# One row's load of a row-wise logsumexp dealt unevenly to the DMA engines, 10, 9, 7 and 6 partitions

## The chip, the cores and the metric

The kernel runs on one core of a Trainium2 chip. The metric is the device time of one execution in microseconds (us). The kernel before takes 162.84 us, the median of three runs (162.67 to 163.0); with the profiled run, 162.7, the result below counts four, and the median is 162.77. A run with the profiler gives a page and a trace; the span there, 161.3 us, goes from the first instruction to the last and is somewhat shorter than the device time.

## The reference

```python
def setup_inputs():
    batch, seq, dim = 32, 512, 1024
    return {"x": np.random.randn(batch, seq, dim).astype(np.float32), "axis": -1}

def reference(x, axis):
    x_max = np.max(x, axis=axis, keepdims=True)
    return (x_max.squeeze(axis) + np.log(np.sum(np.exp(x - x_max), axis=axis))).astype(np.float32)
```

64 MB come in, 64 KB go out. Each of the 128 partitions of the on-chip memory takes 128 rows of 1024 numbers. "A row" below means one such row in every partition: 128 pieces of 4 KB.

## The kernel before

The rows come in chunks, 17 loads in all, into a ring of 51 rows. The last four chunks are single rows.

```python
CHUNKS = [
    (4, 4, 1, False), (15, 15, 1, False), (16, 16, 2, False), (16, 16, 2, False),
    (16, 15, 2, False), (14, 14, 2, False), (13, 12, 2, False), (9, 8, 1, False),
    (7, 7, 1, True), (5, 5, 1, True), (4, 4, 1, True), (3, 3, 1, False), (2, 2, 1, True),
    (1, 0, 1, False), (1, 0, 1, False), (1, 0, 1, False), (1, 0, 1, False),
]
# ... cut ...
    def load(i):
        (s, row), r = place[i], CHUNKS[i][0]
        act_wait = max(a for a, _ in busy[s : s + r])
        dve_wait = max(d for _, d in busy[s : s + r])
        if dve_wait:
            nc.sync.wait_ge(dve_done, dve_wait)
        if act_wait:
            nc.sync.wait_ge(act_done, act_wait)
        nc.sync.dma_start(out=ring[:, s : s + r], in_=x_v[:, row : row + r]).then_inc(
            landed[i], 16
        )
# ... cut: ScalarE takes exp of a chunk, VectorE sums it; of the last four rows ScalarE does both ...
        nc.scalar.wait_ge(landed[i], 16)
        for j in range(n_dve, r):
            nc.scalar.activation(
                out=ring[:, s + j], in_=ring[:, s + j], func=Exp, accum_out=total(row + j),
            ).then_inc(act_done, 1)
```

No maximum is subtracted. At the end the kernel counts the sums that lie in a safe range, and only if one does not, a branch runs a second pass. That part is the same in both kernels.

## Time and profile before

| what | value | where it is from |
|---|---|---|
| span | 161.3 us | head of the page |
| share of the DMA queue, sixteen engines | 97.2% | the page's queue table |
| last increment of the loads of chunks 13, 14, 15, 16 | 154.56, 155.85, 157.13, 158.35 us | semaphore increments in the trace |
| start of the exponential on those rows | 155.28, 156.28, 157.28, 158.37 us | the timeline |

A load of 128 partitions leaves sixteen increments of its semaphore in the trace. Linked end to start, the packets of the last four rows form sixteen chains, one for each of the page's sixteen DMA engines, with eight packets and one increment for each row. So a load leaves sixteen time stamps, and ScalarE, which waits for all of them, starts on the last row 0.02 us after its last one (158.37 against 158.35 us). The lines of the page, the chain, the timeline and the tail of the DMA rate are shown in the prediction below.

### The profile page before, as it was taken

The numbers are of one execution on the slowest core, as the hardware profiler recorded it, in microseconds if no ns is written. First come the engines' busy times: TensorE is split into PE (matmuls) and PEld (weight loads), VectorE is DVE, ScalarE is ACT, GpSimd is POOL, SyncE is SP. The second block draws the span as 40 slices with busy tenths as digits, with TensorE's granted clock in tenths as the row PEclk, the third lists the DMA queues.
The fourth block names the chain that finished last, engine by engine and source line by source line (L and its number), as shares of the span: only waits on it lengthen the run. The fifth ranks groups of instructions, "written<-read, shape, count | busy, mean of one in ns | idle before, by whom it ended". The sixth has DMA issues, their size and how long they took to land.

```text
span 161.3 us, 147 instructions
## 1 busy us (share of the span) xinstructions
PE 0.2 (0%) x1; PEld 0.1 (0%) x1; DVE 123.0 (76%) x57; ACT 114.8 (71%) x36; POOL 0.3 (0%) x5
## 2 busy tenths in 40 slices
PE   0000000000000000000000000000000000000000
PEld 0000000000000000000000000000000000000000
DVE  0019000003999999999999699999999999999994
ACT  3080005996079960999419993999199999999996
POOL 0000000000000000000000000000000000000000
DMA  7998899799899899899899999999999999999990
GB/s 266 500 488 381 381 457 520 341 439 520 358 423 520 358 423 520 374 406 520 358 390 455 455 455 439 423 423 423 403 430 439 423 427 420 422 427 421 404 401 34
DMA packets 2593, 67.18 MB, mean 417 GB/s; under 512 B 288, under 2 KB 416, under 8 KB 928
## 3 DMA queue, kind: packets, MB, share of 16 engines
q1 hardware_dynamic: 2592, 67.18, 97.2%
q14 instruction: 1, 0.01, 0.0%
HBM read 67.11 MB, written 0.07 MB: 416 GB/s over the span
## 4 chain that ended last, share of the span: by engine, by line
DMA 51%; DVE 30%; ACT 17%; issue 1%; SPq 0%; PE 0%
DMA ring<-in_x_dram 51%; DVE sums L182 29%; ACT ring L162 15%; ACT ring L189 2%; SPq L122 0%; DVE counts L222 0%; ACT res L131 0%; PE good L227 0%; DVE n_good L232 0%
## 5 line engine op out<-in xcount | busy, mean ns | idle before, releaser
L182 DVE TENSOR_REDUCE sums<-ring 128x8 f32<-128x8192 f32 (+5 forms) x14 | 111.2, 7995 | 36.3 <-ACT ring L162 36.1
L162 ACT ACTIVATE ring<-ring 128x8192 f32<-128x8192 f32 (+7 forms) x18 | 106.1, 5932 | 43.9 <-DMA ring<-in_x_dram 43.9
L169 DVE CUSTOM_DVE_ANT_0 ring<-ring 128x512 f32<-128x512 f32 x18 | 11.2, 688 | 0.0
L189 ACT ACTIVATE ring<-ring 128x1024 f32<-128x1024 f32 x7 | 7.2, 1045 | 0.0
L149 ACT ACT_TABLE_LOAD x1 | 1.3, 1283 | 1.0 <-PEq L312 1.0
L169 DVE DVE_READ_ACCUMULATOR2_ANT sums<- 128x1 f32 x18 | 1.5, 84 | 0.0
L189 ACT ACTIVATION_READ_ACCUMULATOR ring<-ring 128x1 f32 x7 | 1.2, 170 | 0.0
L222 DVE TENSOR_SCALAR counts<-late 128x4 bf16<-128x4 f32 x2 | 0.2, 156 | 0.8 <-ACT res L131 0.8
L206 DVE TENSOR_SCALAR_CACHE_REDUCE marks<-sums 128x124 bf16<-128x124 f32 x2 | 0.5, 280 | 0.0
L131 ACT ACTIVATE res<-sums 128x81 f32<-128x81 f32 (+1 forms) x2 | 0.5, 242 | 0.0
L232 DVE TENSOR_REDUCE n_good<-good 1x1 int32<-1x10 f32 x1 | 0.2, 155 | 0.3 <-PE good L227 0.3
L227 PE MATMUL good<-counts,ones 128*1 128x10 bf16 x1 | 0.2, 168 | 160.0 <-DVE counts L222 160.0
L131 ACT ACTIVATE res<-late 128x4 f32<-128x4 f32 x1 | 0.2, 173 | 0.0
L206 DVE DVE_READ_ACCUMULATOR marks<-sums 128x1 bf16 x2 | 0.2, 86 | 0.0
L227 PEld LDWEIGHTS good<-counts,ones 128*1 128x1 bf16 x1 | 0.1, 79 | 160.0 <-DVE counts L222 160.0
L148 POOL MEMSET ones<- 128x1 bf16 x1 | 0.1, 101 | 0.5 <-POOLq L312 0.5
L312 POOL MEMSET const-bfloat16-1.0<- 128x1 bf16 x1 | 0.1, 101 | 0.0
L312 POOL MEMSET const-uint8-127<- 128x1 uint8 x1 | 0.1, 101 | 0.0
L312 POOL MEMSET const-float32-0.0<- 128x1 f32 x1 | 0.1, 98 | 0.2 <-issue 0.2
L312 POOL MEMSET const-float32-1.0<- 128x1 f32 x1 | 0.1, 98 | 0.0
## 6 DMA issues: line engine op xcount, KB each, us to landing
ring<-in_x_dram SPq DMA_DIRECT2D x1, 7680.0 KB, 25.0
ring<-in_x_dram SPq DMA_DIRECT2D x1, 7168.0 KB, 28.6
ring<-in_x_dram SPq DMA_DIRECT2D x1, 6656.0 KB, 35.7
ring<-in_x_dram SPq DMA_DIRECT2D x1, 4608.0 KB, 20.3
ring<-in_x_dram SPq DMA_DIRECT2D x2, 2048.0 KB, 16.3
ring<-in_x_dram SPq DMA_DIRECT2D x1, 3584.0 KB, 28.3
ring<-in_x_dram SPq DMA_DIRECT2D x1, 2560.0 KB, 27.4
ring<-in_x_dram SPq DMA_DIRECT2D x4, 512.0 KB, 27.0
```

What stands on the lines that cost most here:

```text
L131: nc.scalar.activation(out=res[:, lo:hi], in_=src, func=Ln).then_inc(act_done, 1)
L148: nc.gpsimd.memset(ones, 1.0).then_inc(early, 1)
L149: nc.scalar.preload_act_table_set("natural_log_exp_and_others")
L162: nc.scalar.activation(out=ring[:, s + lo : s + hi], in_=ring[:, s + lo : s + hi], func=Exp).then_inc(act_done, 1)
L169: nc.vector.tensor_tensor_reduce(out=ring[:, s + j, : D // 2], in0=ring[:, s + j, : D // 2], in1=ring[:, s + j, D // 2 :], scale=1.0, scal ...
L182: nc.vector.reduce_sum(out=sums[:, row + lo : row + hi], in_=ring[:, s + lo : s + hi], axis=AX).then_inc(dve_done, 1)
L189: nc.scalar.activation(out=ring[:, s + j], in_=ring[:, s + j], func=Exp, accum_out=total(row + j),).then_inc(act_done, 1)
L206: nc.vector.tensor_scalar(out=marks[:, c, :late_row], in0=sums[:, :late_row], scalar1=bound, scalar2=None, op0=op, op1=Add, accum_out=coun ...
L222: nc.vector.tensor_scalar(out=counts[:, at : at + LATE], in0=late[:, :LATE], scalar1=bound, scalar2=None, op0=op).then_inc(marked, 1)
L227: nc.tensor.matmul(good[:1, : 2 + 2 * LATE], lhsT=ones, rhs=counts, start=True, stop=True).then_inc(counted, 1)
L232: nc.vector.reduce_sum(out=n_good, in_=good[:1, : 2 + 2 * LATE], axis=AX).then_inc(known, 1)
L312: nc = _bacc.Bacc("TRN2", target_bir_lowering=False, num_devices=1)
```

## The change

Its intent, as I read it: the engines do not finish together, so the row fourth from last is not cut evenly, 8 partitions for each engine, but in six loads. If the loads of 12, 4 and 8 partitions use the engines that the probes of 12, 4 and 8 use, engines 0–3 get 10 partitions, 4–7 get 9, 8–11 get 7 and 12–15 get 6.

```diff
+UNEVEN = (13,)
+PARTS = (
+    (0, 128, 2), (1, 128, 4), (3, 96, 8), (99, 128, 8), (7, 64, 8), (71, 128, 8),
+)
...
-        nc.sync.dma_start(out=ring[:, s : s + r], in_=x_v[:, row : row + r]).then_inc(
-            landed[i], 16
-        )
+        dst, src = ring[:, s : s + r], x_v[:, row : row + r]
+        if i not in UNEVEN:
+            nc.sync.dma_start(out=dst, in_=src).then_inc(landed[i], 16)
+            return
+        for first, last, step in PARTS:
+            nc.sync.dma_start(
+                out=dst[first:last:step], in_=src[first:last:step]
+            ).then_inc(landed[i], 16)
...
-        nc.scalar.wait_ge(landed[i], 16)
+        nc.scalar.wait_ge(landed[i], 16 * (len(PARTS) if i in UNEVEN else 1))
```

## The prediction

> **What bounds the kernel now.** I read the page first, then the chain of waits that ended last, then the timeline of the last ten microseconds, then the DMA view of that stretch, then the issue line.
>
> The page's busy tenths and its queue table:
>
> ```profile
> DVE  0019000003999999999999699999999999999994
> ACT  3080005996079960999419993999199999999996
> DMA  7998899799899899899899999999999999999990
> ...
> q1 hardware_dynamic: 2592, 67.18, 97.2%
> ```
>
> The 64 MB load keeps the DMA queue at 97.2% of 16 engines' span. It never pauses until the last slice, and ScalarE and VectorE run beside it. So bytes set the bulk of the 161.3 us, and nothing in this change touches a byte. What the change can move is how the last rows arrive. The chain of waits, pieces in order of time:
>
> ```profile
> 122.76 28.03 DMA ring<-in_x_dram
> 150.79 0.02 issue
> 150.81 4.56 ACT ring L162 x2
> 155.38 3.04 ACT ring L189 x7
> 158.41 0.92 issue
> 159.33 0.15 ACT ring L189
> 159.49 0.21 ACT res L131 x2
> ```
>
> The last load that truly held the chain is the three-row chunk that lands at 150.79. From there ScalarE works without a break: 4.56 us for chunks 11 and 12, then the four single rows. The loads of those rows (chunks 13 to 16; chunk 13 is the one changed) must beat ScalarE, which the timeline shows:
>
> ```profile
> 155.28 1.04 ACT L189 ACTIVATE ring<-ring 128x1024 f32<-128x1024 f32 x1
> ...
> 156.28 1.04 ACT L189 ACTIVATE ring<-ring 128x1024 f32<-128x1024 f32 x1
> ...
> 157.28 1.05 ACT L189 ACTIVATE ring<-ring 128x1024 f32<-128x1024 f32 x1
> ...
> 158.37 1.06 ACT L189 ACTIVATE ring<-ring 128x1024 f32<-128x1024 f32 x1
> ```
>
> The starts are 1.00, 1.00 and 1.09 us apart. The first three are ScalarE's own pace; only the fourth is late, by 0.09 us. The sixteen semaphore increments of each load stand in the trace one by one. The last of the sixteen comes at 154.56, 155.85, 157.13 and 158.35 us for chunks 13 to 16. The slack against those starts is 0.72, 0.43, 0.15 and 0.02 us. So only the last row's load touches the end, and only just. The page puts the 0.92 us after 158.41 down to "issue"; by these increments it is in truth the last row's own activation.
>
> The DMA view of the window from 150 to 159 us (a slice is 0.225 us) shows why that load ends raggedly:
>
> ```profile
> GB/s 364 328 510 437 437 364 473 382 382 437 328 419 382 455 382 382 437 382 455 382 401 455 346 455 382 419 437 346 473 364 401 310 237 109 36 0 0 0 0 0
> ```
>
> From about 157 us the rate falls in steps, 401, 310, 237, 109, 36: the engines run dry one after another over 1 us. The increments of the last load, sorted, lie at 0, 55, 252, 304, 358, 421, 449, 537, 566, 629, 649, 676, 716, 850, 884 and 984 ns after 157.36. The spread was already 1.02 us at chunk 1, so it is a standing skew between engines, begun at the start (the first packets of the sixteen engines start between 1.00 and 1.76 us) and carried to the end. Dealing one row unevenly is meant to take that out: fewer partitions for the engines that lag, more for those that lead.
>
> [...]
>
> **The change part by part.** Only the load changes. The counted sums and the branch of the title stand in both kernels; on ScalarE, VectorE, TensorE and GpSimd the order of instructions is the same, line numbers aside. The one load of 128 partitions becomes six of 64, 32, 12, 4, 8 and 8 partitions.
>
> Issue cost. The issue line:
>
> ```profile
> L122 SPq DMA_DIRECT2D ring<-in_x_dram x17: 327/372/762, 0.0 to 130.2; - x17
> ```
>
> Five more issues at 0.33 to 0.48 us (the last four stand at that) are 1.7 to 2.4 us on SyncE. Chunk 16 would be issued near 132.5 instead of 130.2 us. Its packets start only near 156 us, behind a queue some 25 us deep, so this is hidden whole.
>
> Deal. [...] the six give each engine of 0–3: 4+2+1+1+1+1 = 10; of 4–7: 4+2+1+1+1 = 9 (no share of the four-partition load); of 8–11: 4+2+1 = 7; of 12–15: 4+2 = 6. Four times 32 is 128, so the row is whole. At 160 ns a partition, against 8, that is +320, +160, −160 and −320 ns.
>
> Extra increments. Engines 0–3 post six increments instead of one, the other groups 5, 3 and 2. A 4-byte increment packet lasts 9 ns in the trace, but the next data packet starts some 5 to 6 ns after it. I take 5 ns each: +25, +20, +10, +5 ns. The shifts are then +345, +180, −150 and −315 ns.
>
> Effect, if the numbering follows the order of arrival (0–3 lead, 12–15 lag). I chose this as the main case because it is the only order for which these numbers make sense. The sorted increments then become 345 to 649, 538 to 717, 416 to 526 and 401 to 669 ns. The last is 717 instead of 984 ns, so chunks 13 to 16 all land 0.27 us earlier, the last at 158.08.
>
> On the path: ScalarE can take the last row only at 157.28 + 1.00 = 158.28 instead of 158.37. Of the 0.27 us, 0.09 reach the end; 0.18 become new slack. Everything after is unchanged, from the end of the last exponential to the last count. Sum: −0.09 us, or 162.84 − 0.09 = 162.75 us.
>
> **The rivals.** (a) Numbering unlike the arrival order. The trace names no engine, so I cannot verify it. If the laggards sit in 0–3, the last increment goes to 984 + 345 = 1329 ns, and with no slack on the last row the end comes 0.33 to 0.35 us later: about 163.2 us. For it: the skew changed between the first and second load, so something other than numbering shaped it. Against it: the deal was clearly written for a known order.
>
> (b) [...] With levelling kept that is 0.64 − 0.27 = 0.37 us later at the last row: about 163.2 us. [...]
>
> (c) Nothing visible. The last landing moves early or late by under 0.1 us, and the time stays at 162.84, the run-to-run range being 162.67 to 163.0. This is not far from the main case in any measurement.
>
> No path gives 2%: that is 3.26 us, and the whole spread of engines is 1 us, with ScalarE 0.09 us behind it.
>
> **Range and chances.** I give the main case and (c) together 0.6, around 162.75 to 162.84, and (a) and (b) together 0.4, around 163.2. The weighted mean is 162.95; the likeliest place is lower, so I say 162.8. For the range I take 162.4 (the lowest run before, 162.67, less the gain, less as much again for another chip or session) to 163.3 (rival (a) or (b) with a little noise). Chances: faster by over 2% 0.01, within 2% 0.98, slower by over 2% 0.01.
>
> **What would show it.** Right: the last four activations on ScalarE start 1.00 us apart with no gap of 0.09; the last load's sixteen increments spread over about 0.4 us, not 1; the rate in the tail falls off in two slices instead of four; SyncE has five more issues, over by about 133 us. Rival (a): the spread grows toward 1.3 us. Rival (b): packets of 4096 bytes clearly above 172 ns (the longest before) in the changed row. I am wrong if the last landing moves and the last activation does not follow, if the four rows' pace on ScalarE changes, or if the queue runs empty while the six loads are issued.

The 160 ns for a packet is the trace's: the packets of the last four rows have a median of 161 ns, eight of which are 1.29 us, and chunks 13 to 15 land 1.28 and 1.29 us apart. Rival (b) was that the strided loads slow each other's packets. For the load of 64 partitions I put this at up to 4 × 160 = 0.64 us, an estimate: four packets of the measured 160 ns, each taking twice as long. That packets would take twice as long, no trace showed. Less the levelling of 0.27 us, its sum came to 0.37 us, about 163.2 us.

## More of the kernel before

One more view of the kernel before is needed later: the DMA view of the stretch from 153.3 to 155.9 us, in which the changed row passes. The line gives packets, bytes and the mean rate.

```profile
DMA packets 294, 1.07 MB, mean 411 GB/s; under 512 B 33, under 2 KB 33, under 8 KB 294
```

In this stretch the rows stream at 411 GB/s.

## The result

The changed kernel takes 163.6 us (median of 4 runs, 163.55 to 163.65) against 162.77 us (4 runs, 162.67 to 163.0): 0.83 us slower. The ratio is 1.0049, 95% interval 1.0031 to 1.0066. Here and below a ratio is the mean time of one kernel's fast runs over that of the other's fast runs of the same rounds, so it is not quite the ratio of the medians that are quoted.

The timeline of the changed kernel, the last four exponentials (start, length, engine, line, operation):

```profile
155.71 1.06 ACT L202 ACTIVATE ring<-ring 128x1024 f32<-128x1024 f32 x1 [0.17 <-DMA ring<-in_x_dram]
156.78 1.06 ACT L202 ACTIVATE ring<-ring 128x1024 f32<-128x1024 f32 x1
158.07 1.06 ACT L202 ACTIVATE ring<-ring 128x1024 f32<-128x1024 f32 x1 [0.17 <-DMA ring<-in_x_dram]
159.30 1.06 ACT L202 ACTIVATE ring<-ring 128x1024 f32<-128x1024 f32 x1
```

They start 1.07, 1.29 and 1.23 us apart. ScalarE now waits for data on these rows. The last increments of chunks 13 to 16 come at 155.69, 156.76, 158.04 and 159.27 us, and each start follows within 0.03 us. The last one is 0.93 us later than in the profile before, and so is the end of the span (162.2 against 161.3).

The chain of waits of the changed kernel, last pieces before the end:

```profile
132.47 0.57 SPq L135
133.04 0.04 issue
133.08 0.44 SPq L130
133.52 0.04 issue
133.56 0.44 SPq L130
134.00 0.04 issue
134.04 25.23 DMA ring<-in_x_dram
159.27 0.02 issue
```

Read literally this puts the blame on SyncE, the engine that issues the loads (SPq in the view): six issues, then three more, and a load that takes 25.23 us from issue to landing. That reading is a trap. The load spends nearly all of the 25 us in the queue, behind the others: the row before it lands only at 158.04 us. The DMA view of the same stretch as above, 153.3 to 155.9 us, tells more (busy tenths of the engines in slices of 0.065 us, then the rate):

```profile
DMA  9299877966994795996989959939959989879796
...
DMA packets 246, 0.87 MB, mean 336 GB/s; under 512 B 33, under 2 KB 33, under 8 KB 246
...
q1 hardware_dynamic: 246, 0.87, 99.4%
```

The engines are occupied (the packets take 99.4% of the sixteen engines' time, last line), yet move 336 GB/s where the kernel before moved 411. Nothing ran dry while waiting for an issue; packets took longer. In the whole trace the 4096-byte packets (those of the last four rows) average 176.7 ns against 162.6, and the longest takes 275 ns against 172.

Two numbers from the increments separate what happened. I call the time from the landing of chunk 10 to that of chunk 14 the passage; the changed row, chunk 13, lies in it. The last engine's passage compares the last increments, the mean passage the means of all sixteen.

| kernel | mean passage, ns | last engine's passage, ns |
|---|---|---|
| before | 8742 | 8740 |
| changed | 9189 | 9486 |
| difference | 447 | 746 |

The deal gives and takes packets in balance, so it cannot move the mean: 447 ns is pure loss on the average engine. It is also what the packets say: 14.05 ns more on each of the 32 packets that an engine has in the last four rows is 450 ns. The last engine loses a further 299 ns, about two packets. The remainder of the 0.93 us in the two profiles, 0.17 us, is already there at chunk 10 (last increment 147.28 against 147.11 us), where both kernels have done the same. I take it for noise of the start: a second profile of the unchanged kernel, below, has 147.54 us there.

### The profile page after: what moved, and what is told of

It is laid out like the page before. It is cut to its first block, busy times and chain, and to the rows that moved or that the text cites. A ratio compares the mean times of both kernels' runs of the same rounds, so it can differ in the third digit from the quotient of the medians.

```text
span 162.2 us, 152 instructions
## 1 busy us (share of the span) xinstructions
PE 0.2 (0%) x1; PEld 0.1 (0%) x1; DVE 123.0 (76%) x57; ACT 115.1 (71%) x36; POOL 0.3 (0%) x5
## 4 chain that ended last, share of the span: by engine, by line
DMA 49%; DVE 33%; ACT 13%; SPq 3%; issue 1%; PE 0%
DMA ring<-in_x_dram 49%; DVE sums L195 33%; ACT ring L175 12%; SPq L135 2%; SPq L130 1%; DVE counts L235 0%; ACT res L144 0%; PE good L240 0%; ACT ring L202 0%; DVE n_good L245 0%
```

## The experiments

Two theories. **Order**: an engine that was last is among those that got more, so it ends two packets later. **Ports**, the name it has in the expectations: the new loads' packets slow each other where they are written. No run here shows ports, so the name stands for no more than that. Rivals: extra issues on SyncE, a bubble at the boundary of each small load, and the read side.

All runs gave outputs that the comparison with the reference accepted. Each is compared with the kernel before in its own rounds (medians 162.78 to 162.96 us); extra_own and extra_foreign ran on another chip than the rest. The changes of the edits are against the changed kernel unless told otherwise. The passages are computed from each run's trace; those of the kernels with an undisturbed row lie between 8742 and 8746 ns in the mean.

| run | median, us | ratio (95%) | mean passage | last passage | mean 4096-byte packet, ns |
|---|---|---|---|---|---|
| before | 162.77 | | 8742 | 8740 | 162.6 |
| changed | 163.60 | 1.0049 (1.0031–1.0066) | 9189 | 9486 | 176.7 |
| before_again | 162.94 | 1.0002 (0.9988–1.0016) | 8746 | 8759 | 162.7 |
| stride_even | 162.92 | 1.0003 (0.9989–1.0017) | 8746 | 8748 | 162.6 |
| src_halves | 162.77 | 0.9993 (0.9977–1.0009) | 8744 | 8747 | 162.6 |
| extra_two | 162.90 | 1.0004 (0.9990–1.0017) | 8784 | 8785 | 162.7 |
| extra_own | 163.17 | 1.0020 (1.0007–1.0034) | 8867 | 9063 | 162.6 |
| extra_foreign | 163.44 | 1.0039 (1.0025–1.0053) | 9181 | 9369 | 172.5 |
| four_even | 163.05 | 1.0014 (1.0000–1.0027) | 9036 | 9054 | 171.0 |
| uneven_spread | 163.58 | 1.0045 (1.0032–1.0059) | 9259 | 9550 | 178.6 |
| dst_halves | 164.88 | 1.0128 (1.0113–1.0144) | 10296 | 10668 | 210.4 |
| halves | 165.00 | 1.0129 (1.0110–1.0148) | 10357 | 10891 | 210.0 |

### Which engine is last: probe_before

Against the kernel before:

```diff
+    for k in range(1, 17):          # after the last row's load
+        nc.sync.dma_start(
+            out=probe[:k, k - 1 : k, :], in_=x_v[:k, k : k + 1, :32]
+        ).then_inc(probed[k - 1], 16)
```

> The kernel before, with sixteen tiny loads behind the last row (to 1, 2, ... 16 partitions, 128 bytes each, each with its own semaphore)[...]. Theory order (lagging engines are among 0-3, which the change gives more): the engine whose increment comes last is among 0-3, or at least not among 12-15. Theory order-as-intended: increments arrive in the order of the numbers, 12-15 last. The time is no measure here; some us of waiting at the end may be added. The last row's increments should spread over about 1.0 to 1.1 us as in the kernel before.

Measured (one look, 163.51 us with the probes' waits at the end): probe k brings k increments. I followed each engine from probe to probe, matching the sorted times; an engine needs 156 to 233 ns from one probe to the next, and each probe adds one engine to those of the probe before. The new one in probe k is called engine k−1; the name says no more than that. In order of arrival at each engine's own first probe, with the distance from the first in ns:

| engine | 6 | 0 | 5 | 2 | 9 | 1 | 4 | 8 | 7 | 11 | 10 | 13 | 15 | 12 | 14 | 3 |
|---|---|---|---|---|---|---|---|---|---|---|---|---|---|---|---|---|
| ns | 0 | 46 | 103 | 111 | 125 | 127 | 156 | 180 | 205 | 342 | 354 | 446 | 454 | 563 | 880 | 931 |

The intended order is nearly there: 0–9 lead, 10–11 follow, 12–15 lag. But engine 3 comes last of all (its increment of the row itself, too, is the last of the sixteen), and it belongs to the group that was given most. The last row's own increments spread over 0.96 us.

### The same in the changed kernel: probe_after

Edit: the probes above, and a semaphore of its own for each of the six loads.

> The changed kernel with the same probes, and with a semaphore of its own for each of the six loads of the changed row. Theory order: the last engine of the last row is among 0-3 and stands about 0.35 us further behind than before the row. Theory ports: engines of all groups lose time in the row, 4096-byte packets average about 177 ns against 163 ns in the kernel before, whatever the group. The last row's increments should spread over about 1.4 us.

Measured (one look, 164.19 us): engine 3 is last again, 980 ns behind the first, and the next is engine 2 at 446 ns. The spread of the last row is 0.98 us, not the 1.4 us expected and seen in the changed kernel's own profile: it grew by 0.15 us from chunk 10, because the leaders lost time as well. The mean passage is 9262 ns, the mean packet 179.0 ns. So both theories hold at once: engine 3 is last, and all engines lose.

Why engine 3? In every one of the fourteen profiles there is one 8 KB packet of the instruction queue 3.4 to 3.6 us into the span, and right behind it one 16 KB packet of the loads takes 1141 ns (1135 in one) where the usual is 611 (some of the very first packets, before 2 us, are as long). Following the packets of each engine from end to start up to chunk 1 (in the twelve traces where that gives sixteen whole chains), the engine that had this packet is the last one at the end of chunk 1 in ten, second in one, third in one. That it is engine 3 was identified in the two probed runs alone; that it is the fetch that makes it last was not tried by removing the fetch.

### Extra packets for engines 0–3, into partitions 0 to 28: extra_own

Against the kernel before; rows 34 and 35 of the ring are free then. The partitions here and in extra_foreign were chosen by which engines I took to write them in a load of 128 partitions; no run here shows that, and "own" and "foreign" in the names of the two runs say no more than which partitions were taken.

```diff
+        if i == 13:
+            for d, (first, last, step) in enumerate(((0, 16, 4), (0, 32, 4))):
+                nc.sync.dma_start(
+                    out=ring[first:last:step, 34 + d], in_=x_v[first:last:step, row]
+                ).then_inc(more, 16)
```

> The kernel before, the row in one even load, plus two extra loads into rows that nobody reads: one partition more for each of engines 0-3, and one more for each of engines 0-7[...]. So engines 0-3 get 2 packets more and 4-7 get 1, 8-15 none, as the deal gives but without taking any away. Theory order: engine 3, the last one, ends 0.32 to 0.36 us later, the end of the kernel 0.25 to 0.36 us later, 163.0 to 163.2 us, and packets stay at 163 ns on average.

Measured: 163.17 us, ratio 1.0020. The last passage grows by 323 ns, two packets of 160; the mean by 125 ns, which is 12 packets over sixteen engines, 120 ns. Packets stay at 162.6 ns. The DMA view of the stretch from 153.3 to 155.9 us:

```profile
DMA packets 300, 1.06 MB, mean 408 GB/s; under 512 B 41, under 2 KB 41, under 8 KB 300
```

This is the deal's share of the loss by itself: 0.32 us on the last engine.

### The same number of extra packets, without engine 3: extra_two

Edit: as before, but both loads are `(0, 8, 4)`, two partitions, so engines 0 and 1, if such a load uses the engines of the probe with two.

> [...] both extra loads go to two partitions (0 and 4), so to engines 0 and 1 alone: 2 packets more each, engine 3 none. Theory order (what costs is that engine 3, the last one, gets more): no change against the kernel before, 162.8 us within 0.15, against 163.2 us where engines 0-3 got the same. Theory that any extra packets or extra loads cost: 163.0 to 163.2 us.

Measured: 162.9 us, ratio 1.0004. Two packets more for engines 0 and 1 cost nothing, and neither do two more loads. It is the last engine's packets that count. With extra_own, where the last passage grew by two packets, this leaves engines 2 and 3 for the last place in runs without probes too: 0 and 1 cost nothing here, and 4–7 got one packet there, 8–15 none.

### The same packets into other partitions: extra_foreign

Edit: as extra_own, with `((99, 128, 8), (71, 128, 8))`.

> The same extra packets for the same engines, but into partitions 99, 107, 115, 123 and 71, 79, ... 127[...]. Theory ports: slower [...] by 0.1 to 0.4 us, packets of 4096 bytes lengthened on engines of all groups. [...]

Both figures were set against extra_own: 0.1 to 0.4 us slower than it by the ports theory, the same as it by order alone.

Measured in the same rounds as extra_own: 163.44 us, ratio 1.0039. The mean passage is 314 ns longer than in extra_own, with the same number of packets; packets average 172.5 ns against 162.6. The same stretch of the DMA view:

```profile
DMA packets 267, 0.94 MB, mean 362 GB/s; under 512 B 37, under 2 KB 37, under 8 KB 267
```

Only the destination and source partitions of the extra packets differ between the two runs, and the rate falls from 408 to 362 GB/s. The times of the two do not overlap (163.00 to 163.26 and 163.31 to 163.61 us).

### Two contiguous halves: halves

```diff
-PARTS = ((0, 128, 2), (1, 128, 4), (3, 96, 8), (99, 128, 8), (7, 64, 8), (71, 128, 8))
+PARTS = ((0, 64, 1), (64, 128, 1))
```

> The same row dealt evenly, 8 partitions to each engine, but as two contiguous loads: partitions 0-63, then 64-127. Theory order: even deal, so no change against the kernel before, 162.8 us, within 0.1. Theory ports: [...] packets of that row last up to 320 ns, and the end comes about 1.0 to 1.3 us later, 163.8 to 164.1 us. Theory issue cost: one more issue, no change.

Measured: 165.0 us, ratio 1.0129; the loss, 2.1 us, is larger than either figure given. Each engine still has 8 partitions, if these loads of 64 are shared out as that of the changed kernel, four to each of sixteen engines. Packets of 4096 bytes last up to 525 ns, and even some of the 8192-byte packets ahead of the row are slowed (up to 942 ns, usual 313). The stretch from 153.3 to 155.9 us:

```profile
DMA  9922989598928992299529945992299429669999
...
DMA packets 181, 0.63 MB, mean 244 GB/s; under 512 B 26, under 2 KB 26, under 8 KB 181
```

The 320 ns of the expectation is twice the measured packet of 160 ns: I had estimated half the rate, on a ground that no run here shows. The trace agrees in direction (244 against 411 GB/s in this stretch).

### Write side or read side: dst_halves and src_halves

The same two halves on one side only, even and odd partitions on the other (the row then holds rows of other partitions; the comparison let it pass, as all results lie close together).

```diff
-                out=dst[first:last:step], in_=src[first:last:step]
+                out=dst[f:l:st], in_=src[f2:l2:st2]
```

> Wrong on purpose for the changed row: two even loads, written to partitions 0-63 then 64-127, but read from even then odd partitions' rows. If the slowness of the two halves is on the write side [...]: about 165 us as with the halves, ratio near 1.013. If it is on the read side: 162.9 us, ratio near 1.000.

> Wrong on purpose for the changed row: two even loads, read from the first then the second half of the rows, but written to even then odd partitions. Write-side theory: 162.9 us, ratio near 1.000. Read-side theory: about 165 us, ratio near 1.013.

Measured: halves on the write side alone give 164.88 us, ratio 1.0128, the same loss. Halves on the read side alone give 162.77 us, ratio 0.9993, no loss. So the slowness of the halves is on the write side (1.0128 against 0.9993). The other cuts were not parted in this way.

### Strides with an even deal: stride_even and four_even

```diff
+PARTS = ((0, 128, 2), (1, 128, 2))                               # stride_even
+PARTS = ((0, 128, 2), (1, 128, 4), (3, 128, 8), (7, 128, 8))     # four_even
```

> The same row dealt evenly, as two strided loads, even and odd partitions: strides as in the change, 8 partitions to each engine. Theory order: no change, 162.8 us within 0.1. Theory ports: packets of the row lengthen as in the change, to some 175 to 185 ns on average over the last rows, and the end comes 0.3 to 0.8 us later, 163.1 to 163.6 us.

> The same row dealt evenly in four strided loads, all over sixteen engines: 4, 2, 1 and 1 partitions each. Theory boundary (each load with one packet per engine costs a bubble, about 0.1 us or more): the end 0.2 to 0.5 us later, 163.0 to 163.4 us. Theory ports/low engines (the loss comes from loads that use only the lowest 4, 8 or 12 engines [...]): no change against the kernel before, within 0.15 us, and 4096-byte packets average 163 ns.

Measured: stride_even 162.92 us, ratio 1.0003, packets unchanged at 162.6 ns: a stride of two costs nothing, against my expectation of the ports theory. four_even 163.05 us, ratio 1.0014; the mean passage is 294 ns longer. I had written that the ports theory expects no change there, which was a miss. The number fits what the boundary theory gave, but the cause does not: the packets themselves lengthen (mean 171.0, longest 355 ns), and 8.3 ns × 32 packets is 267 of the 294 ns. A bubble between loads would leave packets as they are. That the stride of eight is the clash, and not the stride of four, has no run of its own; it rests on the traces alone. With each engine's packets followed from end to start, the first packet above 172 ns begins 0.43 us after the first engine enters a load of stride eight in four_even, 0.47 in the changed kernel and 0.50 in uneven_spread after the load on twelve engines, and 0.44 in extra_foreign after the first extra packet. Counted from the load `(1, 128, 4)` it would be 0.74 to 0.82 us in the first three, and extra_foreign, which has no such load, would need another cause.

The same packets show who pays. In four_even the seven engines that were ahead wrote all eight packets of the changed row in 159 ns each; their slow packets (up to 355 ns) are those of the next row, which is one even load. So here the slowing fell on packets of another load, not only on the strided loads' own. Which engine writes which partition of a strided load, and what makes the packets slow each other, no run here shows.

### A better spread of the last 32 partitions: uneven_spread

```diff
+PARTS = ((0, 128, 2), (1, 128, 4), (3, 51, 4), (51, 67, 4), (67, 99, 4), (99, 128, 4))
```

> The deal of the change, 10, 9, 7 and 6, but the last 32 partitions cut in blocks (every fourth partition, 12, 4, 8, 8 in a row)[...]. Theory deal alone: same as the change, 163.6 us. Theory ports: part of the 0.45 us that all engines lose on average comes back, 0.1 to 0.3 us, so 163.3 to 163.5 us, packets of 4096 bytes averaging 166 to 173 ns.

Measured: 163.58 us, ratio 1.0045, nothing came back; the mean passage is 9259 ns, if anything longer. This was a miss. Cutting the last 32 partitions with a stride of four instead of eight does not help: packets average 178.6 ns against 176.7. The reason was not shown.

### The unchanged kernel once more: before_again

> The kernel before, unchanged, for the noise of the measurement and a second profile of it. All theories: ratio 1.000 within 0.0015; one 16 KB packet near 3.5 us lengthened behind the fetch of instructions, as in every profile so far; the last load's increments spread over 0.8 to 1.1 us.

Measured: 162.94 us, ratio 1.0002. Between the two profiles of this same kernel the last increment of chunk 10 differs by 0.44 us and the spread of the last load is 0.98 and 0.83 us. So a difference of under some 0.4 us between two single profiles says nothing by itself; the passage, which cuts off the start, differs by 4 ns in the mean and 19 ns in the last engine.

No run points to a version that beats the kernel before.

## Why the prediction was wrong

**What held.** The last row is what the end waits for; its slack of 0.02 us meant that any later landing goes through whole, and it did (0.93 us in the landing, 0.93 in the last exponential's start). No 2% either way. The cost of the deal as such, two packets of 160 ns plus little for the increments, is measured in extra_own as 323 ns. The extra issues are hidden: chunk 16 is issued at 134.0 us, not 132.5, because the six loads took 0.56 to 0.87 us each to issue, but this is still more than 20 us ahead of the data.

**The step that failed** is "Effect, if the numbering follows the order of arrival (0–3 lead, 12–15 lag)". The numbering follows the order for most engines, but not for engine 3, which is last in both probed runs (931 and 980 ns behind the first). I reasoned that the deal makes sense only for that order and so took the order as given. A single engine out of order is enough: instead of 267 ns off, the last engine got 323 ns on (measured in extra_own). This is rival (a), close to the size it was given (0.33 to 0.35 us).

**The second error was to weigh rivals (a) and (b) as alternatives.** Both came true, with the signs that the prediction named: the last load's spread grew to 1.41 us, and packets reached 275 ns. Rival (b), loads that slow each other's packets, is in the changed kernel 447 ns on the mean engine, and by subtraction 746 − 323 = 423 ns on the last. I had put it at up to 640 ns less a levelling gain of 270 ns that did not exist. The sum is 0.32 + 0.42 = 0.74 us, against 0.83 us between the medians, an excess of the size of the run-to-run range. With rivals (a) and (b) added instead of averaged, the range would have had to reach 163.6 us (0.34 and 0.37 on top of 162.84), or 163.8 without the levelling.

**A detail of rival (b) was also off.** I expected the strided load of 64 partitions to slow packets. It does not (stride_even, 162.6 ns). What slows them are the loads after it: those of stride eight, as far as the traces tell (four_even, 171.0 ns), and those on eight or fewer engines, depending on the partitions they write (extra_foreign, 172.5 ns, but extra_own 162.6).

**One reading before was too trusting.** The trace showed a lengthened 16 KB packet 3.7 us into the span, and a skew that was not a tidy ladder. I saw that "something other than numbering shaped it" and gave it too little weight.

## What to carry to other kernels

Where the last engine sets the landing, look for who that engine is before dealing work away from it; here the last one, engine 3, was among the engines of every probe with four partitions or more, so such loads could not spare it. Leave a row in one load of 128 partitions unless a run shows that the cut is free: with such loads alone the kernel before has no slowed packets in the last four rows (none above 172 ns), while cuts of the same row cost from nothing (even and odd partitions) to 2.1 us (two halves), against a skew of 1 us that was to be cured. When two rivals can both come true on the same path, add them in the range.
